# Which two of the eight K pairs take seven products: the fourth and the sixth in place of the fifth and the sixth

## The chip, the cores and the metric

The kernel runs on one core of one Trainium2 chip. The metric is the device time of one execution in microseconds (us). Engines are TensorE (PE, with its weight loads PEld), VectorE (DVE), ScalarE (ACT), GpSimd (POOL) and SyncE (SP), which issues the weight transfers.

## The reference

One decoder layer on 256 tokens of width 2048 in float32: two half-step SwiGLU feed-forward nets (FFNs) of hidden width 5632 around a mixer, with RMSNorms before each and at the end.

```
x = x + 1/2 * SwiGLU_1(RMSNorm(x))        # (silu(h @ w_gate) * (h @ w_up)) @ w_down
x = x + mixer(RMSNorm(x))                 # attention and a gated short convolution
x = x + 1/2 * SwiGLU_2(RMSNorm(x))
out = RMSNorm(x)
```

The change touches the two FFNs alone.

## The kernel before, in words

**Products in parts.** Every float32 operand is split into a high part (a rounding to fp32r) and a low part (the rest). One product of two 128x512 blocks is then three matmuls, in `product`: L230 high by high, L231 high by low, L232 low by high. The weights are streamed from HBM; ACT makes the high part `hi` (L907) and DVE the low part `lo` (L908), both in `cut`. There are four buffers of each, so the cut of a chunk can start when TensorE has finished the chunk four places before it.

**Groups and pairs.** Most of an FFN is done in groups (`group`). A group multiplies 256 tokens (two halves of 128) by two column blocks of 512 weights, over a depth of 2048, and has four accumulators in PSUM (tile `pv`). The depth is taken in eight K pairs of 2 x 128 rows, the first to the eighth. An ordinary pair is 2x2 blocks by 2x2 blocks in eight products: two chunks of weights, 12 matmuls each. In the pairs named by `FAST` (L30, counted from zero) the same 2x2 by 2x2 product is done with seven products of sums of blocks (Winograd's form of Strassen's scheme). A fast pair is four chunks: `a` (6 matmuls), `b` (3), `s1` (6), `s2` (6). For `b` and `s1` DVE adds weight blocks into `usum`, a part of the tile `sacc` (L880, two adds each), and `s1` and `s2` are split from there. The products of `s1` go to the PSUM tiles `psS` and then `psT`, the first one of `s2` to `psV`; these three banks and one more are kept from the first fast pair to the last, and are then read by DVE and ACT in the eighth pair and just before it.

**Order.** Everything is in an order written by hand. When TensorE's code asks for a chunk, `advance` puts the cut of the chunk three places later into the queues of ACT and DVE. After each chunk `flush` takes one item of `pending` and `tick` goes on with the `turns`: a turn transposes a part of the hidden vector on TensorE into one of `psS`, `psT`, `psV` (step A, L323), splits it into `ring` (step B, L330 and L331), and, where the part belongs to a fast pair of a later group, forms sums of it (step C, L301 to L304) and splits these (step D, L309). `hold_banks` keeps transposes out of the three banks; it is set in the pair before the first fast pair and lifted in the eighth:

```
if fast and p == fast[0] - 1 and n == 0:
    hold_banks(True)
```

An FFN runs the gate and up groups g0, u0, g1, u1, g2, then a down group pair, u2, g3, u3, g4, a down pair, u4, and some blocks without fast pairs. g0 has no fast pairs. So an FFN has 13 groups with fast pairs (u0 to u4, g1 to g4, four down groups) and the kernel 26. Turns of hidden parts run in the group behind each up group, that is in g1 to g4.

Of the kernel before, what the change touches and what calls it, by code (L numbers as in the profile page):

```python
# [26 lines left out]
NB = D // NW  # L27
GK = 4
WARM = 11
FAST = (4, 5)  # L30
RING = 16
LOAD_AHEAD = 6
SPLIT_AHEAD = 4
# [18 lines left out]
def macaron_kernel(ctx: ExitStack, tc: tile.TileContext, xt, gf, cst, wg1, wu1, wd1, win, wv, wao,  # L52
# [22 lines left out]
    def ring(k):  # L75
        return phase["ring"][:, k, :]
# [17 lines left out]
    def vec(off, i):  # L94
        return cs[:, off + i:off + i + 1]
# [193 lines left out]
    def sums_at(base):  # L289

        return lambda q: {m: (at[:, base + 2 * q, j * P:(j + 1) * P], at[:, base + 2 * q + 1, j * P:(j + 1) * P])
                          for j, m in enumerate((5, 6, 3, 7))}

    H_SUMS, X_SUMS = 0, 2 * len(FAST)

# [96 lines left out]
    def turn_x(tag, m, goff):  # L392
# [3 lines left out]
        def scale():  # L396
            for i in range(2):
                nc.vector.tensor_scalar(xs[:, i, :], x[:, i, m * P:(m + 2) * P], scale0[tag][:, i:i + 1], None,
                                        op0=ALU.mult)
        slot = X_SUMS + 2 * FAST.index(m // 2) if m // 2 in FAST else None  # L400
        return turn(lambda q, i: xs[:, i, q * P:(q + 1) * P], xn[:, m:m + 2, :], lambda q: vec(goff, m + q), slot,
# [135 lines left out]
    def ffn(tag, wg, wu, wd, gain_next, next_tag):  # L537
# [17 lines left out]
        def hidden(q, t):  # L555

            k0 = next(a for a, b in ROUNDS if a <= t < b)
            p = (t - k0) // 2
            slot = H_SUMS + 2 * FAST.index(p) if p in FAST and k0 != ROUNDS[-1][0] else None
            r = t % RING  # L560
# [7 lines left out]
        def gu(which, b):  # L568
            fast = () if (which, b) == ("g", 0) else FAST
            use = gate if which == "g" else up  # L570

            def drain(C, n):
                assert which == "u" or not any(t[1][0][0] in "SA" for t in turns)
                if which == "g" and b == 0 and n == 0:
                    exact_over_rough_once(tag)
                for i in range(2):
                    src = C[i, n]
                    if fast:
                        q, op = sign[i, n]
                        nc.vector.tensor_tensor(part[q], C[i, n], part[q], op=op)  # L580
                        src = part[q]
                    use(i, src, slice(n * NW, (n + 1) * NW))
                if which == "u":
                    for q in (2 * n, 2 * n + 1):
                        hidden(q, 8 * b + 2 * q)
            w = wg if which == "g" else wu
            steps.append(group(w[2 * b], w[2 * b + 1], 0, ND // 2, lambda k: xn[:, k, :], fast, sums_at(X_SUMS),
                               parts_of, drain))
# [13 lines left out]
        def down(r):  # L602
            k0, k1 = ROUNDS[r]
            for n1 in (0, 2):
# [12 lines left out]
                def drain(C, n, cols=cols):  # L617
                    for i in range(2):
                        into(i, cols[n], C[i, n], 0.5)
                steps.append(group(wd[n1], wd[n1 + 1], k0, (k1 - k0) // 2, lambda k, k0=k0: ring((k0 + k) % RING),  # L620
                                   FAST, sums_at(H_SUMS), early, drain))

# [441 lines left out]
```

## Time and profile before

| | |
|---|---|
| median of 3 runs | 2493.36 us (2493.25 to 2493.5) |
| profiled execution, its own time | 2493.28 us |
| span of that execution in the trace | 2491.5 us |
| PE busy | 2451.4 us, 98% |
| DVE busy | 1763.4 us, 71% |
| ACT busy | 1216.7 us, 49% |
| HBM traffic | 187 GB/s over the span, weight queue 58.5% |

The profiled execution lasts 1.78 us longer than its span. The shares are means over the whole span; the mixer in the middle and the FFNs at both ends load DVE differently.

### The profile page before, as it was taken

To read this page: it belongs to the slowest core of one execution; us is meant where nothing else is said; L and a number is where in the kernel's file an instruction comes from. 1 tells how busy PE (TensorE), PEld (TensorE's weight loads), DVE (VectorE), ACT (ScalarE), POOL (GpSimd) and SP (SyncE) were. 2 spreads that over 40 slices of the span, in tenths; PEclk is the share of its full clock that TensorE was granted. 3 is DMA by queue.
4 is the path that set the end of the run, shared out by engine and by line. 5 is a ranking of instruction groups with operands and counts; after the bars stand their busy time and mean duration, and the time that the engine had idled before them with its cause. 6 is when DMAs were issued, how large, how long until landed. Compare 5 with 4: busy or idle time off the path is not lost.

```text
span 2491.5 us, 31739 instructions
## 1 busy us (share of the span) xinstructions
PE 2451.4 (98%) x12030; PEld 2063.2 (83%) x12030; DVE 1763.4 (71%) x2290; ACT 1216.7 (49%) x1573; POOL 1.9 (0%) x10
## 2 busy tenths in 40 slices
PE   9999999999999999999999999999999999999998
PEld 7878788787888888888888888888887878878787
DVE  6778787978657777655556566666578888787865
ACT  5455444544455444444445455445545544454544
POOL 0000000000000000000000000000000000000000
PEclk9999999999999999999999999999999999999999
DMA  7555565565656555555555545566656556565664
GB/s 229 186 191 193 176 209 189 186 201 177 203 156 205 197 189 191 189 193 188 187 175 171 177 159 195 187 194 186 186 177 203 186 183 205 170 203 188 194 198 155
DMA packets 130841, 468.76 MB, mean 188 GB/s; under 512 B 14464, under 2 KB 14720, under 8 KB 130688
## 3 DMA queue, kind: packets, MB, share of 16 engines
q1 hardware_dynamic: 130256, 466.15, 58.5%
q8 instruction: 94, 1.54, 0.3%
q10 hardware_dynamic: 432, 0.59, 0.1%
q14 instruction: 59, 0.48, 0.1%
HBM read 464.58 MB, written 2.10 MB: 187 GB/s over the span
## 4 chain that ended last, share of the span: by engine, by line
PE 92%; DVE 5%; ACT 1%; issue 1%; DMA 0%; ACTq 0%; DVEq 0%
PE ps L165 21%; PE pv L232 14%; PE pv L230 14%; PE pv L231 14%; PE ps L166 11%; PE pv L194 3%; PE pv L192 3%; PE pv L193 3%; DVE sacc L880 3%; DVE lo L908 2%; ACT hi L907 1%; PE pv L744 1%; PE pv L745 1%; PE pv L746 1%; PE psS L231 1%
## 5 line engine op out<-in xcount | busy, mean ns | idle before, releaser
L908 DVE TENSOR_TENSOR lo<-w,hi 128x1024 fp32r<-128x1024 f32 (+2 forms) x883 | 1031.9, 1183 | 548.7 <-ACT hi L907 544.2
L907 ACT CAST hi<-w 128x1024 fp32r<-128x1024 f32 (+2 forms) x883 | 885.6, 1017 | 719.4 <-PE pv L232 411.9
L165 PE MATMUL ps<-xn,hi 128*128 128x512 f32 x1744 | 611.8, 394 | 0.0
L166 PE MATMUL ps<-xn,lo 128*128 128x256 f32 x1744 | 487.9, 280 | 0.0
L230 PE MATMUL pv<-hi,xn 128*128 128x512 f32 x1228 | 483.2, 394 | 0.5 <-ACT pv L124 0.4
L231 PE MATMUL pv<-lo,xn 128*128 128x512 f32 x1228 | 478.6, 390 | 0.9 <-DVE lo L908 0.9
L232 PE MATMUL pv<-hi,xn 128*128 128x512 f32 x1228 | 479.0, 390 | 0.0
L165 PEld LDWEIGHTS ps<-xn,hi 128*128 128x128 f32 x1744 | 327.6, 188 | 71.5
L166 PEld LDWEIGHTS ps<-xn,lo 128*128 128x128 f32 x1744 | 327.7, 188 | 0.5
L232 PEld LDWEIGHTS pv<-hi,xn 128*128 128x128 f32 x1228 | 230.6, 188 | 48.7 <-DVE xn L106 0.2
L230 PEld LDWEIGHTS pv<-hi,xn 128*128 128x128 f32 x1228 | 230.7, 188 | 48.1 <-ACT pv L124 0.8
L231 PEld LDWEIGHTS pv<-lo,xn 128*128 128x128 f32 x1228 | 230.8, 188 | 47.9 <-DVE lo L908 1.2
L907 ACT CAST hi<-sacc 128x1024 fp32r<-128x1024 f32 x104 | 109.3, 1051 | 175.0 <-DVE sacc L880 131.8
L908 DVE TENSOR_TENSOR lo<-sacc,hi 128x1024 fp32r<-128x1024 f32 x104 | 127.2, 1223 | 62.2 <-ACT hi L907 60.8
L232 PE MATMUL pv<-hi,ring 128*128 128x512 f32 x432 | 168.2, 389 | 0.0
L230 PE MATMUL pv<-hi,ring 128*128 128x512 f32 x432 | 168.2, 389 | 0.0
L231 PE MATMUL pv<-lo,ring 128*128 128x512 f32 x432 | 168.2, 389 | 0.0
L192 PE MATMUL pv<-hi,ring 128*128 128x512 f32 x304 | 120.3, 396 | 0.0
L194 PE MATMUL pv<-hi,ring 128*128 128x512 f32 x304 | 118.7, 391 | 0.0
L193 PE MATMUL pv<-lo,ring 128*128 128x512 f32 x304 | 118.5, 390 | 0.0
L231 PEld LDWEIGHTS pv<-lo,ring 128*128 128x128 f32 x432 | 81.1, 188 | 16.9
L230 PEld LDWEIGHTS pv<-hi,ring 128*128 128x128 f32 x432 | 81.1, 188 | 16.9
(198 smaller groups left out, 2528.2 us busy)
## 6 DMA issues: line engine op xcount, KB each, us to landing
w<-in_win SPq DMA_DIRECT2D x218, 512.0 KB, 4.1
w<-in_wu SPq DMA_DIRECT2D x176, 512.0 KB, 4.2
w<-in_wd SPq DMA_DIRECT2D x176, 512.0 KB, 4.1
w<-in_wg SPq DMA_DIRECT2D x175, 512.0 KB, 4.1
w<-in_wco SPq DMA_DIRECT2D x32, 512.0 KB, 4.0
w<-in_wv SPq DMA_DIRECT2D x32, 512.0 KB, 4.2
w<-in_wao SPq DMA_DIRECT2D x32, 512.0 KB, 4.5
w<-in_wo SPq DMA_DIRECT2D x32, 512.0 KB, 3.8
```

The source lines that it names most:

```text
L165: nc.tensor.matmul(ps, hi[:, j * P:(j + 1) * P], r, start=(k == 0), stop=False)
L166: nc.tensor.matmul(ps[:, 0:T], lo[:, j * P:(j + 1) * P], r[:, 0:T], start=False, stop=(k == n - 1))
L192: nc.tensor.matmul(pv, xh, hi[:, cols], start=start, stop=False)
L193: nc.tensor.matmul(pv, xh, lo[:, cols], start=False, stop=False)
L194: nc.tensor.matmul(pv, xl, hi[:, cols], start=False, stop=stop)
L230: nc.tensor.matmul(ps, xh, hi[:, sl], start=start, stop=False)
L231: nc.tensor.matmul(ps, xh, lo[:, sl], start=False, stop=False)
L232: nc.tensor.matmul(ps, xl, hi[:, sl], start=False, stop=stop)
L744: nc.tensor.matmul(pv[i], xh, hi[:, cols], start=(k == 0), stop=False)
L880: nc.vector.tensor_add(dst, a, b)
L907: nc.scalar.copy(hi[:, cols], w[:, cols])
L908: nc.vector.tensor_sub(lo[:, cols], w[:, cols], f32(hi[:, cols]))
```

## The change

The constant that names the fast pairs goes from (4, 5) to (3, 5), counted from zero: the fourth and the sixth of the eight pairs are fast, with one ordinary pair (the fifth) between them.

```
-FAST = (4, 5)
+FAST = (3, 5)
```

Which rows of x and of the hidden vector get sums follows from the same constant (L400, L559), and so does the place where the three banks are held. The number of instructions that compute is the same. The order of the weight transfers on SP is the same.

In the queue of DVE, in u0 (the first group with fast pairs), from the cuts of its ordinary pairs on: `lo<-w` is the cut of a chunk of weights, `sacc<-w` and `sacc<-sacc,w` the adds for `b` and `s1`, `lo<-sacc` the cut of `s1` or `s2`. Before:

```order
L908 TENSOR_TENSOR lo<-w,hi 128x1024 x7
L880 TENSOR_TENSOR sacc<-w 128x512 x2
L908 TENSOR_TENSOR lo<-w,hi 128x512
L880 TENSOR_TENSOR sacc<-sacc,w 128x512 x2
L908 TENSOR_TENSOR lo<-sacc,hi 128x1024 x2
L908 TENSOR_TENSOR lo<-w,hi 128x1024
L880 TENSOR_TENSOR sacc<-w 128x512 x2
L908 TENSOR_TENSOR lo<-w,hi 128x512
L880 TENSOR_TENSOR sacc<-sacc,w 128x512 x2
L908 TENSOR_TENSOR lo<-sacc,hi 128x1024 x2
L908 TENSOR_TENSOR lo<-w,hi 128x1024 x4
```

And now, in the same place:

```order
L908 TENSOR_TENSOR lo<-w,hi 128x1024 x5
L880 TENSOR_TENSOR sacc<-w 128x512 x2
L908 TENSOR_TENSOR lo<-w,hi 128x512
L880 TENSOR_TENSOR sacc<-sacc,w 128x512 x2
L908 TENSOR_TENSOR lo<-sacc,hi 128x1024 x2
L908 TENSOR_TENSOR lo<-w,hi 128x1024 x3
L880 TENSOR_TENSOR sacc<-w 128x512 x2
L908 TENSOR_TENSOR lo<-w,hi 128x512
L880 TENSOR_TENSOR sacc<-sacc,w 128x512 x2
L908 TENSOR_TENSOR lo<-sacc,hi 128x1024 x2
L908 TENSOR_TENSOR lo<-w,hi 128x1024 x4
```

Two cuts of an ordinary pair have moved from ahead of the first fast pair to between the two.

In the queue of DVE, in g1, where the last two turns of the hidden vector meet the first fast pair (`ring` is step B, the `c` rows step C, `at<-c` step D), as it stands now:

```order
L331 TENSOR_TENSOR ring<-psT,ring 128x2x256
L880 TENSOR_TENSOR sacc<-w 128x512 x2
L908 TENSOR_TENSOR lo<-w,hi 128x512
L331 TENSOR_TENSOR ring<-psV,ring 128x2x256
L880 TENSOR_TENSOR sacc<-sacc,w 128x512 x2
L908 TENSOR_TENSOR lo<-sacc,hi 128x1024
L301 TENSOR_TENSOR c_1044<-psV,a 128x128
L302 SCALAR_TENSOR_TENSOR c_1044<-c_1044,a 128x128
L303 TENSOR_TENSOR c_1044<-psV,c_1044 128x128
L304 TENSOR_TENSOR c_1044<-a 128x128
L908 TENSOR_TENSOR lo<-sacc,hi 128x1024
L309 TENSOR_TENSOR at<-c_1044,at 128x512
```

Before, g1 and g3 formed no sums and g2 and g4 two each, clear of the fast pairs; now each of the four forms one, and in g1 and g3 it lies between the cuts of `s1` and `s2` of the fourth pair.

## Rows read from the trace of the kernel before

**Rows 1.** The page's first lines: span; busy time, share and instructions by engine.
```profile
span 2491.5 us, 31739 instructions
...
PE 2451.4 (98%) x12030; PEld 2063.2 (83%) x12030; DVE 1763.4 (71%) x2290; ACT 1216.7 (49%) x1573; POOL 1.9 (0%) x10
```

**Rows 2.** Waits of PE, whole span: total us, times, longest us.
```profile
PE psS L231 <- DVE lo L908: 27.6, 26, 1.3
...
PE pv L231 <- DVE lo L908: 0.9, 1, 0.9
```

**Rows 3.** Timeline of PE in g1: start us, us, instruction [idle before <- releaser].
```profile
115.91 0.60 PE L323 MATMUL psV<-ident,gbuf 128*128 128x128 f32 x4
...
128.62 0.39 PE L230 MATMUL pv<-hi,at 128*128 128x512 f32 x1
...
129.53 0.39 PE L231 MATMUL psS<-lo,at 128*128 128x512 f32 x1
...
130.89 0.39 PE L231 MATMUL psV<-lo,at 128*128 128x512 f32 x1
...
131.34 0.39 PE L230 MATMUL pv<-hi,xn 128*128 128x512 f32 x1
...
134.06 0.39 PE L230 MATMUL psS<-hi,at 128*128 128x512 f32 x1
135.50 0.50 PE L231 MATMUL psS<-lo,at 128*128 128x512 f32 x1 [1.05 <-DVE lo L908]
135.84 0.40 PE L232 MATMUL psS<-hi,at 128*128 128x512 f32 x1
136.07 0.39 PE L230 MATMUL psT<-hi,at 128*128 128x512 f32 x1
```

**Rows 4.** Timeline of DVE in g1.
```profile
117.19 1.23 DVE L908 TENSOR_TENSOR lo<-w,hi 128x1024 fp32r<-128x1024 f32 x1 [1.38 <-ACT hi L907]
...
125.87 1.22 DVE L908 TENSOR_TENSOR lo<-sacc,hi 128x1024 fp32r<-128x1024 f32 x1 [1.12 <-ACT hi L907]
128.59 1.23 DVE L908 TENSOR_TENSOR lo<-sacc,hi 128x1024 fp32r<-128x1024 f32 x1 [1.50 <-ACT hi L907]
129.95 1.22 DVE L908 TENSOR_TENSOR lo<-w,hi 128x1024 fp32r<-128x1024 f32 x1
131.09 1.29 DVE L880 TENSOR_TENSOR sacc<-w 128x512 f32<-128x512 f32 x2
132.30 0.68 DVE L908 TENSOR_TENSOR lo<-w,hi 128x512 fp32r<-128x512 f32 x1
132.90 1.41 DVE L880 TENSOR_TENSOR sacc<-sacc,w 128x512 f32<-128x512 f32 x2
134.23 2.50 DVE L908 TENSOR_TENSOR lo<-sacc,hi 128x1024 fp32r<-128x1024 f32 x2
```

**Rows 5.** Timeline of ACT in g1.
```profile
127.50 1.05 ACT L907 CAST hi<-sacc 128x1024 fp32r<-128x1024 f32 x1 [1.67 <-PE pv L232]
128.86 1.57 ACT L907 CAST hi<-w 128x1024 fp32r<-128x1024 f32 x2 [0.31 <-PE pv L232]
132.49 1.06 ACT L907 CAST hi<-sacc 128x1024 fp32r<-128x1024 f32 x1 [2.05 <-DVE sacc L880]
```

**Rows 6.** Timeline of DVE in g2, where turns form sums.
```profile
202.31 0.28 DVE L301 TENSOR_TENSOR c<-psS,a 128x128 f32<-128x128 f32 x1
...
203.36 0.68 DVE L331 TENSOR_TENSOR ring<-psT,ring 128x512 fp32r<-128x512 f32 x1
...
206.57 0.68 DVE L309 TENSOR_TENSOR at<-c,at 128x512 fp32r<-128x512 f32 x1
```

**Rows 7.** DMA issues by line: count, KB each, median us from issue to landing.
```profile
w<-in_wu SPq DMA_DIRECT2D x176, 512.0 KB, 4.2
```

## The prediction

> **What bounds the kernel now.** I read the busy table first: TensorE is busy 2451.4 of 2491.5 us and every other engine much less [rows 1], so only what shortens TensorE's 40.1 us of idleness, or its own work, can help. The number of matmuls does not change. Next the table of what TensorE waits for: one line holds most of the idle time, 26 waits of the second matmul of `s1`, into `psS`, for DVE's low part, 27.6 us together [rows 2]. The kernel has 26 groups with fast pairs and 52 fast pairs, so half of the fast pairs wait. Which half is seen in the timeline of g1 [rows 3]. The first fast pair (the fifth) runs its matmul into `psS` at 129.53 and that into `psV` at 130.89 with no idle time in front; the second fast pair (the sixth) starts `psS` at 134.06 and its next matmul only at 135.50, after 1.05 us of idleness.
>
> The cause is in DVE's queue [rows 4]. Between 129.95 and the end of the last cut at 134.23 + 2.50 = 136.73 it works without a gap on one fast pair: a cut of `a` (1.14 from start to start), two adds (1.21), the short cut of `b` (0.60), two adds (1.33), and two cuts (2.50), 6.8 us in all. TensorE takes 21 matmuls for a fast pair. From 131.34 to 134.06 there are 12 steps in 2.72 us, 0.227 each [rows 3], so a fast pair is 4.77 us and an ordinary one, of 24 matmuls, 5.45. DVE loses 2.0 us to TensorE in each fast pair. It regains 5.45 - 2 x 1.14 = 3.2 in an ordinary one, up to the lead that four buffers allow. Two fast pairs in a row ask for a lead of almost 4.0, and it is short by 1.05.
>
> **The change, part by part.**
>
> *The wait itself.* What one wait costs TensorE is more than the idle time shown. From 134.06 to 135.84 are two steps, which take 0.454 elsewhere and 1.78 here [rows 3]: 1.33 us, 0.28 above the 1.05 of idleness. If all 26 go: 27.6 + 26 x 0.28 = 34.9 us. (That the twenty-odd matmuls behind the wait keep step again is seen at 136.07, 0.23 after 135.84.)
>
> The row shows this price of a restart as 0.28 [rows 3]. The Trainium skill, "TensorE: Matmul & The Clock Gate", sections "Single matmul latency" and "Back-to-back issue gap", gives a lone warm matmul of N columns (398 + N)/2.4 ns and one in a stream N/2.4 + 2.5 ns; at 512 columns these are 379 and 216, so a restart would cost 0.16 above the idle time. By it the sum would be 27.6 + 26 x 0.16 = 31.8 us and the time 2461.5. I go by the row, which also holds the slower step after the late matmul.
>
> *Whether the sixth pair now finds its low parts.* I lay the new order out from the start of the first fast pair's `a` chunk, which today is 128.62 - 6 x 0.227 = 127.26 [rows 3]. TensorE then reaches `s2` at 3.41, the fifth pair at 4.77 and 7.49, the sixth's `a` at 10.22, `b` at 11.58, `s1` at 12.26 and its matmul with the low part at 12.49; that of `s2` comes at 13.85. DVE starts the cut of the first pair's `s2` at 1.33 and the next cut at 2.69 (128.59 and 129.95 today [rows 4]). From there, with today's distances: two cuts of the fifth pair to 4.97, `a` to 6.11, adds to 7.32, `b` to 7.92, adds to 9.25, and the cut of `s1` to 10.5. That is 2.0 us before TensorE wants it; today it is 1.05 late. ACT is no tighter: its casts wait for TensorE's buffers, not for its own work [rows 5].
>
> *What is late next.* The cut of `s2`. Its cast waits for the buffer that TensorE frees at the start of `a`, 0.24 later (127.50 against 127.26 [rows 5]), and DVE starts 1.33 after that start and is done at 2.56, whichever pair it is. TensorE wants it at 3.63 (130.89 [rows 3]). This margin of 1.07 is the one that the fifth pair has today and does not miss. So every fast pair should now look like today's fifth.
>
> *The fourth pair, 5.45 us earlier in the group than today's first fast pair.* DVE must have caught up from the group's start by then. Today it waits for ACT, and ACT for TensorE, already three chunks ahead: 1.38 idle before 117.19, and 1.12 and 1.50 before the cuts of `s1` and `s2` [rows 4]. In the 18 groups without turns there is less to do still. I take nothing; bounds: no gain is possible from it, and if all of the margin of 1.07 were eaten each us beyond it costs one us per group.
>
> *The turns.* The banks are held one pair sooner, so the four transposes of g1 to g4 have to be issued within the first four chunks. They are already: the last of them ends the fourth chunk, at 115.91 [rows 3], before the third pair. They stay where they are. The sums of step C take 1.05 us of DVE (202.31 to 203.36) and step D 0.68 [rows 6]. There are eight of each before and after, but in g1 and g3 (four groups of the kernel) step C now stands before the cut of `s2` of the fourth pair. There DVE is idle for 1.50 us today [rows 4], and C's inputs are old; it fits. Step D comes behind that cut, and delays the cuts of the fifth pair by 0.68: the first is done at 2.69 + 0.68 + 1.22 = 4.6, wanted at 4.77 + 0.23 = 5.0. That is the tightest place I find, 0.4 us. If it fails, it fails in four groups: from 0 to 4 x (0.68 + 0.28) = 3.8 us; I take 0. In g2 and g4 one sum fewer stands ahead of the fast pairs than today, but these begin 5.45 us earlier; the nearest row is the last split of a turn (0.68), and my bound is eight groups late by one C and one D less the margin, 1.05 + 0.68 - 1.07 = 0.66, with the restart 0.94 each, 7.5 us; I take 0, since each chunk of an ordinary pair leaves DVE about 2.72 - 1.14 = 1.6 us.
>
> *Sums of x, transfers.* The sums for the fourth pair rather than the fifth are formed one turn earlier in g0, which has no fast pairs; nothing. The transfers keep their order on SP. A load waits for the buffer five places back, and lands 4.2 us after issue [rows 7]. Two adjacent fast pairs use up two buffers each until their adds are done; with a pair between, the last adds (9.25) free buffers for a chunk cut after 15.0, more room than today. Nothing.
>
> **Sum.** 2493.28 - 34.9 = 2458.4 us against the profiled execution; the median of the runs shown is 0.08 above it, so 2458.5. Of TensorE's 40.1 us of idleness 12.5 remain; the 0.9 us wait for a low part in `pv` [rows 2] is among them, and none of it is touched.
>
> **Rivals.** (A difference of 0.2%, 5 us, is about what a measurement can tell from none.)
>
> *A. The waits go in most groups, and smaller ones come in those with turns.* For it: the 0.4 us margin above, and the strict order of C and D among the cuts. Against it: the idle time of 1.50 in just this place. Price: up to 7.5 us in g1 to g4: 2466.
>
> *B. The sixth pair waits as before,* because DVE does not regain its lead in one ordinary pair. It would need DVE 2.0 us later than laid out. For it: DVE's total over the three pairs, 2 x 6.8 + 2.3 = 15.9, is above TensorE's 2 x 4.77 + 5.45 = 15.0. Against it: the deficit of 0.9 is below the lead that bore almost 3 today. If half the wait stays, 2493.3 - 17 = 2476; if all, 2493.
>
> *C. Slower: the fourth pair becomes late too.* Place: its matmuls into `psS` and `psV`, right after the splits of the turns and the drains of the previous group on DVE. If DVE reached it as late as it reaches today's sixth, every group would have two waits of 1.33 where it has one: 2493.3 + 34.9 = 2528. The point from which it decides is DVE arriving there over 1.07 us behind; to end slower than today the fourth pair must lose over 1.33 us per group with the sixth's wait gone. Against it: DVE idles 1.38 us before 117.19, at the chunk where the fourth pair's cuts would begin [rows 4].
>
> **How the numbers follow.** The forecast gets 0.80, with its own range from 2456 to 2462 (a restart cost of 0.37 or of 0.14 per wait in place of 0.28). A gets 0.09 (2462 to 2470), B 0.07 (2470 to 2493, half of it within 5 us of today), C 0.04. The range 2456 to 2468 leaves out about 0.15. Faster by over 0.2%: 0.80 + 0.09 + 0.035 = 0.92; the same 0.04; slower 0.04.
>
> **What the changed profile would show.** Right: the line of 26 waits for `lo` at `psS` is gone or down to a few; TensorE's busy share is 99% or more with idle time near 12.5 us (40.1 - 27.6); DVE shows idle time for ACT before the cuts of `s1` and `s2` in both fast pairs. Step D wrong: waits of `pv` L231 in the fifth pair of g1 and g3, four in number. B: the 26 waits stand, shorter, at the second `psS`. C: waits at the first `psS` or `psV` of a group. The forecast fails if any wait of 26 or more times shows in PE's table.

## The result and the profile after

The changed kernel takes 2457.2 us (2457.06 to 2457.24, 4 runs) against 2493.31 us before (2493.24 to 2493.5, 4 runs): a ratio of 0.9855 with a 95% interval of 0.9838 to 0.9872, or 36.1 us less. The prediction was 2458.5 us, in a range from 2456 to 2468.

The page's first lines of the changed kernel answer to [rows 1]:

```profile
span 2455.4 us, 31711 instructions
...
PE 2442.7 (99%) x12030; PEld 2064.3 (84%) x12030; DVE 1763.6 (72%) x2290; ACT 1221.7 (50%) x1573; POOL 1.9 (0%) x10
```

The work is the same: DVE's busy time stays at 1763 us. TensorE's idle time falls from 40.1 to 2455.4 - 2442.7 = 12.7 us, 27.4 less, and its busy time falls by 8.7 as well, though it runs the same matmuls. What TensorE waits for, to be read against [rows 2]:

```profile
PE psS L323 <- DVE gbuf L398: 1.7, 1, 1.7
PE psS L954 <- DVE gbuf L951: 1.2, 1, 1.2
PE pv L231 <- DVE lo L908: 0.9, 1, 0.9
PE pv L230 <- ACT pv L124: 0.4, 1, 0.4
```

The line of 26 waits is gone and no line of many waits has come in its place. Of the four that are left, each a single wait, three lie in the first 20 us and the last one (0.4 us) between mixer and second FFN.

Timelines of u0, a group without turns: TensorE at the first matmul of `s1` of the fourth pair, at the first two of `s1` of the sixth, and at the low-part matmul of its `s2`; then DVE from the cut of the fourth pair's `s2` on:

```profile
78.33 0.39 PE L230 MATMUL psS<-hi,at 128*128 128x512 f32 x1
...
88.53 0.39 PE L230 MATMUL psS<-hi,at 128*128 128x512 f32 x1
88.76 0.39 PE L231 MATMUL psS<-lo,at 128*128 128x512 f32 x1
...
90.12 0.39 PE L231 MATMUL psV<-lo,at 128*128 128x512 f32 x1
```

```profile
77.62 1.22 DVE L908 TENSOR_TENSOR lo<-sacc,hi 128x1024 fp32r<-128x1024 f32 x1 [1.49 <-ACT hi L907]
78.98 3.50 DVE L908 TENSOR_TENSOR lo<-w,hi 128x1024 fp32r<-128x1024 f32 x3
82.39 1.29 DVE L880 TENSOR_TENSOR sacc<-w 128x512 f32<-128x512 f32 x2
83.60 0.68 DVE L908 TENSOR_TENSOR lo<-w,hi 128x512 fp32r<-128x512 f32 x1
84.20 1.41 DVE L880 TENSOR_TENSOR sacc<-sacc,w 128x512 f32<-128x512 f32 x2
85.53 1.22 DVE L908 TENSOR_TENSOR lo<-sacc,hi 128x1024 fp32r<-128x1024 f32 x1
87.82 1.22 DVE L908 TENSOR_TENSOR lo<-sacc,hi 128x1024 fp32r<-128x1024 f32 x1 [1.07 <-ACT hi L907]
```

In the sixth pair the cut of `s1` ends at 85.53 + 1.22 = 86.75, 2.0 us ahead of the matmul at 88.76; before, it ended some 1.05 us too late [rows 3]. DVE has even 1.07 us of idle time before the cut of `s2`, which ends 1.08 ahead of its matmul (89.04 against 90.12). Where DVE worked without a gap before [rows 4], it now waits ahead of `s2` for ACT's cast, and that cast for a buffer that TensorE frees, as ACT's row of the same cast in g1 shows:

```profile
130.83 1.05 ACT L907 CAST hi<-sacc 128x1024 fp32r<-128x1024 f32 x1 [1.51 <-PE pv L232]
```

In g1 the sums of a turn (L301 to L304) stand between the two cuts, as laid out. DVE, and then TensorE at the low-part matmul of the fifth pair's first chunk:

```profile
119.00 1.23 DVE L908 TENSOR_TENSOR lo<-sacc,hi 128x1024 fp32r<-128x1024 f32 x1 [0.91 <-ACT hi L907]
120.14 0.28 DVE L301 TENSOR_TENSOR c<-psV,a 128x128 f32<-128x128 f32 x1
...
121.71 1.23 DVE L908 TENSOR_TENSOR lo<-sacc,hi 128x1024 fp32r<-128x1024 f32 x1 [0.44 <-ACT hi L907]
122.85 0.69 DVE L309 TENSOR_TENSOR at<-c,at 128x512 fp32r<-128x512 f32 x1
123.46 3.49 DVE L908 TENSOR_TENSOR lo<-w,hi 128x1024 fp32r<-128x1024 f32 x3
```

```profile
125.37 0.39 PE L231 MATMUL pv<-lo,xn 128*128 128x512 f32 x1
```

DVE still has 0.44 us to spare before the cut of `s2`, so the sums cost TensorE nothing. The fifth pair's first cut ends near 123.46 + 1.22 = 124.68, 0.7 ahead of its matmul. The sixth pair's cut of `s1` is 1.6 ahead in this group (it starts at 130.00, for the matmul at 132.85).

### The profile page after: what moved, and what is told of

It is laid out like the page before. It is cut to its first block, busy times and chain, and to the rows that moved or that the text cites. A ratio compares the mean times of both kernels' runs of the same rounds, so it can differ in the third digit from the quotient of the medians.

```text
span 2455.4 us, 31711 instructions
## 1 busy us (share of the span) xinstructions
PE 2442.7 (99%) x12030; PEld 2064.3 (84%) x12030; DVE 1763.6 (72%) x2290; ACT 1221.7 (50%) x1573; POOL 1.9 (0%) x10
## 4 chain that ended last, share of the span: by engine, by line
PE 99%; DVE 0%; ACT 0%; DMA 0%; issue 0%; DVEq 0%
PE ps L165 21%; PE pv L230 16%; PE pv L232 16%; PE pv L231 16%; PE ps L166 11%; PE pv L194 3%; PE pv L193 3%; PE pv L192 3%; PE pv L744 1%; PE pv L745 1%; PE pv L746 1%; PE psV L231 0%; PE psT L231 0%; PE psS L231 0%; PE psS L232 0%; PE psV L232 0%
## 5 line engine op out<-in xcount | busy, mean ns | idle before, releaser
L231 PE MATMUL pv<-lo,xn 128*128 128x512 f32 x1228 | 478.2, 389 | 0.9 <-DVE lo L908 0.9
L231 PEld LDWEIGHTS pv<-lo,xn 128*128 128x128 f32 x1228 | 230.7, 188 | 47.8 <-DVE lo L908 1.2
L231 PE MATMUL pv<-lo,ring 128*128 128x512 f32 x432 | 168.1, 389 | 0.0
L231 PEld LDWEIGHTS pv<-lo,ring 128*128 128x128 f32 x432 | 81.1, 188 | 16.9
```

Source lines behind the costliest of these rows:

```text
L231: nc.tensor.matmul(ps, xh, lo[:, sl], start=False, stop=False)
```

## The experiments

The theory: DVE loses about 2 us to TensorE in a fast pair; two in a row use up its lead, and one ordinary pair between restores enough of it. The main rival: it is not the spacing but the place, the first fast pair being earlier and the sums of the turns elsewhere. All times stand beside the kernel before at 2493.3 us and the changed one at 2457.2 us.

**e1_34: early, but adjacent.**

```
-FAST = (3, 5)
+FAST = (3, 4)
```

> The fast pairs are the fourth and the fifth: as early as in the changed kernel, but next to each other. Theory (VectorE needs an ordinary pair between two fast ones to regain its lead): the 26 waits of about 1.05 us at the second matmul of s1 in the second fast pair are back, 26 x 1.39 = 36 us, so 2493 us, within 3. Rival (it is the earlier place of the first fast pair, or where the sums of turns now lie, that helps): no waits, 2457 us.

Measured: 2494.43 us (ratio to before 1.0005, 0.9995 to 1.0014). The waits are back, in the same number:

```profile
PE psS L231 <- DVE lo L908: 28.8, 26, 1.4
```

The earlier place of the first pair gives nothing by itself. The sixth place of the second pair does not either, since the kernel before has it too. What is left is the ordinary pair between, as expected.

**e3_45less: the pairs as before, with less of DVE's work ahead of the cut.**

```
+fasts = [0]
 ...
 if kind == "b":
     a, b = raw[c - 1], w
-    add(usum[:, 0:NW], a[:, 0:NW], b[:, 0:NW])
-    add(usum[:, NW:2 * NW], b[:, 0:NW], b[:, NW:2 * NW])
+    fasts[0] += 1
+    if fasts[0] % len(FAST):
+        add(usum[:, 0:NW], a[:, 0:NW], b[:, 0:NW])
+        add(usum[:, NW:2 * NW], b[:, 0:NW], b[:, NW:2 * NW])
     ...
```

`fasts` counts the fast pairs, and only the first of each two makes the sums for `b`. The kernel leaves out sums that the second needs, so it does not compute the layer; it is there for its time.

> The kernel before (fifth and sixth pair fast), but the two adds for b of each second fast pair are left out, so its products use the sums of the first one. That takes 1.2 us from VectorE ahead of the cut of s1, where TensorE waited 1.05 us. Theory: the waits are gone, or below 0.2 us each, without any move: 2457 to 2463 us. Rival (place of the pairs, or the order of sums and turns): 2493 us.

Measured: 2462.06 us (0.9875, 0.986 to 0.9889). TensorE's table of waits has no line at `psS` L231. So 1.2 us less of DVE's work, and no move, takes away 31.3 of the 36.1 us. What is left, 4.9 us or 0.19 per group, has no idle time of TensorE beside it. It shows in the waits of its weight loads, and in the timeline of one such pair:

```profile
PEld psS L231 <- DVE lo L911: 7.3, 26, 0.6
```

```profile
132.66 0.39 PE L230 MATMUL psS<-hi,at 128*128 128x512 f32 x1
132.90 0.50 PE L231 MATMUL psS<-lo,at 128*128 128x512 f32 x1
133.23 0.40 PE L232 MATMUL psS<-hi,at 128*128 128x512 f32 x1
```

The matmul starts in step (0.24 after the one before it), but lasts 0.50 where others last 0.39, and the next one comes 0.33 later and not 0.23. These two steps lose 0.12 us and the ten behind them 0.05. The low part came in time for the matmul, but too late for its weights to be loaded ahead: this load starts at 132.90 with its matmul, where the load before it starts 0.22 ahead of its own (132.44 against 132.66).

**e4_add2 and e5_add4: the changed kernel with more of DVE's work at this place (1.3 and 2.6 us were expected, 1.5 and 2.9 measured).** The two adds of `s1` are repeated once or, in e5_add4 with `range(2)`, twice in each second fast pair; the sums do not change.

```
+fasts = [0]
 ...
 add(usum[:, 3 * NW:4 * NW], usum[:, 2 * NW:3 * NW], a[:, NW:2 * NW])
+fasts[0] += 1
+if fasts[0] % len(FAST) == 0:
+    for _ in range(1):
+        add(usum[:, 2 * NW:3 * NW], usum[:, 0:NW], b[:, NW:2 * NW])
+        add(usum[:, 3 * NW:4 * NW], usum[:, 2 * NW:3 * NW], a[:, NW:2 * NW])
```

> The changed kernel with two of the adds repeated in each second fast pair, 1.3 us more of VectorE ahead of the cut of s1, 26 times. Theory (a lead of 2.0 us at this cut, 1.6 in the groups with a sum just before it): all of it is covered, 2457.2 us within 0.7. Rival (VectorE's work on fast pairs counts in proportion): up to 26 x 1.3 = 34 us more, 2470 to 2491 us.

> The changed kernel with four more adds in each second fast pair, 2.6 us of VectorE ahead of the cut of s1. Theory (lead of 2.0 us at this cut, 1.6 in the four groups with a sum just before it): late by 0.6 in 22 groups and by 1.0 in 4, each with 0.2 to 0.33 us for the restart, 22 x 0.9 + 4 x 1.3 = 25 us: 2482 us, within 6, with 26 waits at the second psS. Rival (the lead is larger than laid out, since ScalarE and the buffers set it): 2457 us again.

Measured: e4_add2 2457.27 us (0.9856, 0.9839 to 0.9872), which is the changed kernel's time; e5_add4 2487.45 us (0.9977, 0.9967 to 0.9986), with the line

```profile
PE psS L231 <- DVE lo L914: 21.9, 26, 1.2
```

and DVE's adds in g1

```profile
129.69 4.31 DVE L881 TENSOR_TENSOR sacc<-sacc,w 128x512 f32<-128x512 f32 x6
```

So 52 adds more cost nothing and 104 more cost 30 us: a margin with an edge, not a price in proportion to DVE's work. Six adds take 4.31 us there, so an extra one takes 0.73 us and not the 0.65 of the expectation, and four are 2.9 us. Less the margin of 2.0 (1.6 in the four groups like g1) that is 0.9 to 1.3 late; measured are 0.84 of idle time on average and 1.2 at most. So the lead is no larger than laid out, and the time lies in the range that was expected.

**e2_36: two ordinary pairs between.**

```
-FAST = (3, 5)
+FAST = (3, 6)
```

> The fast pairs are the fourth and the seventh, with two ordinary pairs between. Theory: one ordinary pair was enough, a second adds nothing, 2457 us within 1.5, no line of 26 waits. Rival (the place of the second pair counts, since the reads of the three banks now fall together with the drain of the four accumulators): new waits at the start of the next group or in the eighth pair, 0.5 us or more in 26 groups, 2470 us or more.

Measured: 2501.23 us (1.0033, 1.002 to 1.0046), slower than before. The theory on spacing alone was wrong here and the rival right. TensorE's waits:

```profile
PE pv L230 <- DVE x L600: 18.0, 8, 2.2
PE pv L230 <- DVE sacc L580: 11.8, 18, 1.1
```

No wait at `psS` L231 is left, but 26 new waits stand at an accumulator, one for each group with fast pairs: 18 of them behind gate and up groups (L580) and 8 behind down groups (L600). The end of g1 on DVE, and TensorE in the group behind it:

```profile
139.14 4.65 DVE L908 TENSOR_TENSOR lo<-w,hi 128x1024 fp32r<-128x1024 f32 x4
143.71 0.68 DVE L543 TENSOR_TENSOR sacc<-psV,sacc 128x512 f32<-128x512 f32 x1
144.43 0.69 DVE L544 TENSOR_TENSOR sacc<-psS,sacc 128x512 f32<-128x512 f32 x1
145.04 0.68 DVE L545 TENSOR_TENSOR sacc<-psT,sacc 128x512 f32<-128x512 f32 x1
145.75 0.69 DVE L546 TENSOR_TENSOR sacc<-psS,sacc 128x512 f32<-128x512 f32 x1
146.36 1.28 DVE L580 TENSOR_TENSOR sacc<-pv,sacc 128x512 f32<-128x512 f32 x2
149.38 1.23 DVE L908 TENSOR_TENSOR lo<-w,hi 128x1024 fp32r<-128x1024 f32 x1 [1.74 <-ACT hi L907]
150.52 1.28 DVE L580 TENSOR_TENSOR sacc<-pv,sacc 128x512 f32<-128x512 f32 x2
```

```profile
151.26 0.50 PE L230 MATMUL pv<-hi,xn 128*128 128x512 f32 x1 [1.05 <-DVE sacc L580]
```

With the last fast pair at the seventh place, the four reads of the banks (L543 to L546) have no ordinary pair to lie beside. They stand in one row ahead of the drain of the accumulators (L580), and the next group wants the third accumulator before it is drained. In the down groups the reads and the adds into x (L600) stand in such a row, from 320.69 on ahead of the wait that ends at 326.14. In the changed kernel the same drain starts at 147.98 and ends near 148.6, for the chunk at 148.94:

```profile
147.98 1.28 DVE L580 TENSOR_TENSOR sacc<-pv,sacc 128x512 f32<-128x512 f32 x2
```

```profile
148.94 0.39 PE L230 MATMUL pv<-hi,xn 128*128 128x512 f32 x1
```

So the drain is on time by 0.3 us there. After a fast pair at the sixth place two ordinary pairs follow, after one at the seventh a single one, in which the reads and the drain fall together. It is this that costs, not the second ordinary pair between the fourth and the seventh. The sum comes out by an estimate: 29.8 us of idle time in these waits, 26 restarts of 0.33 us (the table below) and five falls of the clock of 1.6 us (the last section) are 46.4 us, and the span is 2500.6 - 2455.4 = 45.2 us longer than the changed kernel's.

**e6_246: three fast pairs in every group.**

```
-FAST = (3, 5)
+FAST = (2, 4, 6)
 ...
 if st:
+    hold_banks(True)
 ...
-if fast and p == fast[0] - 1 and n == 0:
-    hold_banks(True)
```

`st` marks the first fast pair, so the banks are held from that pair on and no longer from the one before it.

> Three fast pairs in every group, the third, the fifth and the seventh, with one ordinary pair between each two; the banks are held from the first fast pair on and not from one pair before it. Three matmuls fewer in 26 groups are 26 x 3 x 0.227 = 17.7 us. Theory on spacing alone: no waits at psS, 2440 us. Theory with what the pairs four and seven showed (reads of the banks and the drain of the accumulators in the same chunks): waits of 1.1 us at the start of the next group in 18 groups and 2.2 in 8, as there, 2440 + 44 = 2484 us. I expect the second.

Measured: 2506.53 us (1.0056, 1.0039 to 1.0072). The same two lines as in e2_36 lead its waits (17.9 us in 8, 11.7 in 18), here with one ordinary pair between each two of the fast pairs: it is the seventh place that brings them. With them come 11.1 us in 6 waits at `psS` and `psT` for the split and the sums of turns (L330 and L302 there), since their banks are asked for a pair sooner, and 2.2 us in 4 waits at `psV` for low parts. The expectation of 2484 named the drain and missed these ten waits, 13.3 of the 22.5 us between; the rest was not traced.

**e7_135: three fast pairs where no turns run.**

```
-FAST = (3, 5)
+FAST = (1, 3, 5)
+GATE_FAST = (3, 5)
 ...
-X = xsum(fast.index(p))
+X = xsum(FAST.index(p))
 ...
-fast = () if (which, b) == ("g", 0) else FAST
+fast = () if (which, b) == ("g", 0) else GATE_FAST if which == "g" else FAST
 ...
-del turns[0:2]
+turns[0:2] = [t for t in turns[0:2] if t[1]]
```

The last line keeps a turn of the start that still has sums to form, since the second pair of x now has some.

> Three fast pairs, the second, fourth and sixth, in the up and down groups (18 of 26); the gate groups g1 to g4, in which the turns run, keep the fourth and the sixth. 18 x 3 x 0.227 = 12.3 us fewer of TensorE. Theory (a fast pair needs a lead of VectorE, which one ordinary pair restores, and nothing else of weight lies in its way): no new waits, 2445 us within 3. Rival (the drain of the previous group, 2.8 to 5.6 us of VectorE, lies ahead of the second pair and eats its lead): waits at the first psS or psV of these 18 groups, up to 1.4 us each, up to 2470 us.

Measured: 2446.99 us (2446.93 to 2447.05; ratio to before 0.9814, 0.9799 to 0.9829), 10.2 us less than the changed kernel, of the 12.3 expected. Its waits:

```profile
PE psS L324 <- DVE gbuf L399: 1.5, 1, 1.5
PE psV L324 <- DVE gbuf L399: 1.4, 1, 1.4
PE psS L955 <- DVE gbuf L952: 1.2, 1, 1.2
PE pv L232 <- DVE lo L909: 0.8, 1, 0.8
PE pv L231 <- ACT hi L908: 0.5, 1, 0.5
PE pv L231 <- ACT pv L125: 0.4, 1, 0.4
```

None comes from the 18 groups with a third fast pair; the drain ahead of the second pair does no harm. The 2 us that are missing lie in the first 20 us, with the two waits that are new, 1.4 and 0.5 us: there DVE forms the sums for the second pair of x (14.22 to 15.28) ahead of what the next transposes need, and the transposes that start at 19.02 in the changed kernel start at 20.91 here, 1.9 us later. This kernel beats both.

## Why the prediction was right

*The bound and the cause.* One fast pair that finds DVE ahead and one that finds it late: e1_34 and e3_45less show this from both sides. With adjacent fast pairs the 26 waits stand at both places tried (fifth and sixth, fourth and fifth), and 1.2 us less of DVE's work takes them away without a move.

*Whether the sixth pair finds its low parts.* The layout put the cut of the sixth pair's `s1` at 9.25 us after the start of the fourth pair and TensorE's need of it at 12.49. In u0 that start is 78.33 - 9 x 0.227 = 76.29; the cut starts at 9.24 and the matmul at 12.47. The margin of 2.0 is confirmed in use by e4_add2 and e5_add4, which lie on either side of it.

*What is late next, the turns.* The margin of 1.07 at `s2` measured 1.08. That every fast pair would look like the fifth of the kernel before was too much: there the cut of `s1` ended 2.4 us ahead (125.87 + 1.22 against 129.53 [rows 3, rows 4]), in the sixth pair now 2.0, and DVE has no idle time before this cut, which was named as a sign for both fast pairs. The lead is full again only at `s2`. In g1 the sums fitted, and step D left 0.7 us where 0.4 was laid out, since it follows the cut of `s2` at once (122.85 is 2.47 us into the pair, and 2.69 was laid out); rival A had nothing in it. The tightest place in the groups looked at was one that the prediction did not look at: the drain of the accumulators, 0.3 us ahead in g1. The change leaves it in place, so this did no harm, but e2_36 shows that with the last fast pair one place later it costs more than the change gives.

*The fourth pair, and rival C.* The row at 117.19, given as the chunk where the fourth pair's cuts begin, is its second chunk. Its first is the cut before that, with the same idle time ahead of it, so the conclusion stands:

```profile
113.98 1.23 DVE L908 TENSOR_TENSOR lo<-w,hi 128x1024 fp32r<-128x1024 f32 x1 [1.38 <-ACT hi L907]
```

*The price of a wait.* This term was sized a little low: 34.9 against 36.1 us. Per wait, over the 26 (the cost is the time above 2457.2 us; the idle time is from the tables of waits):

| kernel | idle, us | cost, us | cost above idle, us |
|---|---|---|---|
| before | 1.06 | 1.39 | 0.33 |
| e1_34 | 1.11 | 1.43 | 0.32 |
| e5_add4 | 0.84 | 1.16 | 0.32 |
| e3_45less | 0 | 0.19 | 0.19 |

The prediction had 0.28 from two steps of the timeline, and took the matmuls behind them to be in step at 0.23 us. They are not quite: the rest is in the dozen steps behind. In the kernel before, twelve steps lead from 136.07 [rows 3] to this row:

```profile
138.85 0.39 PE L230 MATMUL pv<-hi,xn 128*128 128x512 f32 x1
```

They take 2.78 us, where twelve of 0.227 would take 2.72. The 8.7 us that went from TensorE's busy time are this part of the price, 26 times about 0.33, which no table of waits shows.

The estimate from the two formulas of the Trainium skill ("TensorE: Matmul & The Clock Gate", "Single matmul latency" and "Back-to-back issue gap"), the first of which is given there for bf16, was 0.16. The measurement is twice that, and it decides.

*Rivals B and C.* Neither happened. B's deficit of 0.9 us over three pairs was borne by the lead, as argued: 1.5 us more of DVE's work did not break it (e4_add2), and 2.9 us more did (e5_add4).

## What to carry to other kernels

Where one engine prepares work for another from a few buffers, a heavy piece is paid from the lead and a light piece restores it: count both in microseconds per piece, and set the heavy ones so far apart that the lead covers the next one. Here 2.0 us of margin were enough, though it was not quite full. Before moving a piece to the end of a loop, look for what else is queued there; the wait that a move removes can return at the loop's drain, as in e2_36. And a wait's price was the idle time plus a restart of about 0.33 us here, so size it from the distance between starts, not from the idle column.

## What the runs showed of the hardware that was not expected

A weight operand that arrives in time for its matmul, but not for the load ahead of it, costs 0.19 us with no idle time anywhere in TensorE's row (e3_45less). Behind a real wait it is 0.32 to 0.33 us.

In e2_36 eight waits are 2.25 us long (18.0 / 8), and the granted clock falls behind five of them: it is 0.91 or 0.95 in the stretches of 20 us that hold these five, and 1.00 in those that hold the other three. What tells the five from the three stays open. Behind the wait that ends at 326.14 it is seen close up; the columns are the stretch, busy us of PE, PEld, DVE, ACT and POOL (count), the granted clock, DMA share and GB/s:

```profile
324.00:326.00 2.00, 0.00 (x0) 0.00 (x0) 1.97 (x5) 0.29 (x1) 0.00 (x0) 1.00 0.18 74
326.00:328.00 2.00, 1.86 (x7) 1.53 (x8) 2.00 (x4) 0.00 (x0) 0.00 (x0) 0.84 0.02 4
328.00:330.00 2.00, 2.00 (x7) 1.52 (x6) 2.00 (x3) 0.63 (x1) 0.00 (x0) 0.50 0.57 135
330.00:332.00 2.00, 2.00 (x9) 1.61 (x8) 1.37 (x2) 0.41 (x1) 0.00 (x0) 0.81 0.69 203
```

TensorE had stood still for 2.25 us, went on for five steps at 0.23 to 0.33 us, and then ran eight steps of 0.41 to 0.43 us, with the granted clock at 0.50, the 1.2 GHz level, before it was back at 0.23: 1.6 us more than the wait itself. The waits of about 1 us in the kernel before, 26 of them, left its mean granted clock at 0.999, as it is in the changed kernel; in e2_36 it is 0.995.
